# HGRN scores by 64 x 64 blocks on quarters of TensorE's array, kept compact and spread before the output

## The chip, the cores and the metric

The kernel runs on one core of a Trainium2 chip. A core has engines that work side by side: TensorE (PE; its weight loads are PEld in the profile), VectorE (DVE), ScalarE (ACT), GpSimd (POOL), and SyncE (SP), whose queue issues the transfers here. The metric is the device time of one execution in microseconds; the median of several runs is compared.

## The reference

Two layers of an encoder on a sequence of 1024 tokens with 1024 features, in float32. In each layer one combined projection feeds three branches: attention (8 query heads, 2 key heads), a bidirectional HGRN2 recurrence (4 heads with a 64 x 64 state), and a convolution module. Their outputs are concatenated and projected back, and an MLP follows. The change is in the HGRN branch, which for each head and each direction computes

```
S_t = diag(f_t) S_{t-1} + k_t outer v_t
o_t = S_t^T q_t
```

with a forget gate f_t per feature. The forward and the backward result are added, normalised and gated. Within a chunk of tokens the result of one direction is a masked product: the score of query i with key j is the sum over features of q_i k_j times all the f between them, and the output is scores times v.

## The kernel before

The kernel is written for a scheduler that takes the order of the code as priorities and decides the final order of each engine's instructions and the place of every buffer when the program is built. The engines then run these orders as they stand; an instruction at the head of a queue that waits holds all that is behind it.

All activations lie features by tokens: 128 partitions (features) by 1024 tokens. An HGRN tile holds two heads, rows 0 to 63 and rows 64 to 127, so a layer has two objects, `Hgrn(0)` and `Hgrn(1)`, that I call head pair 0 and head pair 1. `Hgrn.__init__` takes its columns of the projection (L223 is the line of all dense matmuls) and leaves q, k and the gates of both directions in `X` (four arrays: key forward in 0, query backward in 1, query forward in 2, key backward in 3) and `T` (the products of f).

`core` is a generator. It doubles the length over which decay is folded in, from 1 token to 128. Ahead of each step s = 2, 4, 8, 16, 32, 64 (`LEVELS`), `scores` computes the scores between the two halves of every block of 2s tokens, for the forward direction in one half of the mask and for the backward one in the other:

- ScalarE (L490) puts the queries and keys of the level together in `qx` and `kx`.
- TensorE (L502) multiplies, for each of eight chunks of 128 tokens and each of the two heads, a full 128 x 128 block from the head's 64 rows. Of it only the pairs of that level are wanted. The eight chunks are done in two halves, each into a pair of PSUM banks, one bank for each head. Head pair 0 takes "c" banks for the first half and "e" banks for the second; head pair 1 takes the two "e" banks both times.
- VectorE merges each bank into the score array `A` (two heads x 8 chunks x 128 queries) under the level's mask: L509 (a product) on the first level, L513 (a predicated copy) on the others.

After that GpSimd and VectorE fold the gates of this length into `X` (L533) and `T` (L534). When all levels are done, TensorE turns the keys (L547), ScalarE copies them out (L548), `U` gathers the products of keys and values per chunk (L557), VectorE runs the states over the chunks (L566), and L591 adds, for each chunk, scores times values and states times queries.

Head pair 0 is interleaved with the projections of attention's q, k and v (`qkv`, L223) and with the convolution's taps on VectorE (L357). Head pair 1 is interleaved with attention: one step of its generator after every second unit of 64. A unit is a head and 128 queries: scores on TensorE (L753), a scaled reduction on VectorE (L764), the exponential on ScalarE (L767), a division on GpSimd (L769), flips on TensorE (L790) which ScalarE and VectorE copy out (L794, L795), and value matmuls (L811), which take one of the same two "e" banks for four units at a time. L199 and L200 split the weights of the dense matmuls into two parts; L819 copies values out of a bank.

Of the kernel before, what the change touches and what calls it, by code (L numbers as in the profile page):

```python
# [17 lines left out]
P = 128  # L18
# [27 lines left out]
def tile_hybrid_trunk(  # L46
# [56 lines left out]
    def pse():  # L103
        return psum.t([P, 512], "e", bufs=2)
# [8 lines left out]
    cons = cst.t([P, 260], "cons")  # L113
    masks = cst.t([P, len(LEVELS), P], "masks", dt=U8)
    ident = cons[:, 0:128]
# [176 lines left out]
    for l in range(DEPTH):  # L292
# [114 lines left out]
        class Hgrn:  # L407
# [76 lines left out]
            def scores(self, lev):  # L484
# [3 lines left out]
                for dst, arrs in ((qx, (1, 2)), (kx, (0, 3))):  # L488
                    for hf in range(2):
                        nc.scalar.activation(  # L490
                            dst.rearrange("p (n h s) -> p n h s", h=2, s=s)[:, :, hf],
                            X[:, arrs[hf]].rearrange("p (n h s) -> p n h s", h=2, s=s)[:, :, hf],
                            AF.Copy,
                        )
                for g in range(2):
                    scs = [pse(), pse()] if g == 1 or self.ls == 1 else [psc(), psc()]
                    for q in range(4):
                        c = g * 4 + q
                        cs = slice(c * P, (c + 1) * P)
                        for hh in range(2):  # L500
                            rows = slice(64 * hh, 64 * hh + 64)
                            nc.tensor.matmul(  # L502
                                scs[hh][:, q * P : (q + 1) * P], kx[rows, cs], qx[rows, cs], start=True, stop=True
                            )
                    for hh in range(2):
                        dst = self.A[:, hh, g * 4 : g * 4 + 4, :]
                        src = scs[hh].rearrange("p (a b) -> p a b", a=4)
                        if lev == 0:
                            nc.vector.tensor_tensor(  # L509
                                dst, src, masks[:, 0].unsqueeze(1).to_broadcast([P, 4, P]), op=ALU.mult  # L510
                            )
                        else:
                            nc.vector.copy_predicated(  # L513
                                dst, masks[:, lev].unsqueeze(1).to_broadcast([P, 4, P]), src
                            )
                    yield

            def core(self):
                ls, X, T, vt = self.ls, self.X, self.T, self.vt
                self.A = hg.t([P, 2, 8, P], "A")  # L520
                yield from self.near()
# [30 lines left out]
                for d in range(2):  # L552
                    U = pse()
                    for c in range(8):
                        for hh in range(2):
# [3 lines left out]
                                start=True, stop=True,  # L559
                            )  # L560
                    step = 1 if d == 0 else -1
                    c = 0 if d == 0 else 7
# [9 lines left out]
                for g in range(2):  # L572
                    op = pse()
                    for q in range(4):
                        c = g * 4 + q
                        cs = slice(c * P, (c + 1) * P)
                        for i in range(3):
                            for hh in range(2):
                                rows = slice(64 * hh, 64 * hh + 64)
                                dst = op[rows, q * P : (q + 1) * P]  # L580
                                if i == 0:
                                    a, b = vt[:, c, rows], self.A[:, hh, c, :]
                                elif i == 1:
# [32 lines left out]
        if l == 0:  # L616
            mraw = x8((P, len(LEVELS), P))
            nc.sync.dma_start(mraw, mask_d)
            nc.vector.tensor_copy(masks, mraw)
# [600 lines left out]
def host_layout(inputs):  # L1220
# [37 lines left out]
    for ax, pos in ((0, t // 64), (1, t % 64)):  # L1258
        ang = (inv[:, None] * pos[None, :].astype(np.float32)).astype(np.float32)
        cs, sn = np.cos(ang.astype(np.float64)), np.sin(ang.astype(np.float64))  # L1260
        for hd in range(2):
            b = hd * 64 + ax * 32
            rope[0, b : b + 16], rope[0, b + 16 : b + 32] = cs, cs
            rope[1, b : b + 16], rope[1, b + 16 : b + 32] = -sn, sn
    i = np.arange(P)
    masks = np.zeros((P, len(LEVELS), P), np.float32)
    for n, s in enumerate(LEVELS):
        same = (i[:, None] // (2 * s)) == (i[None, :] // (2 * s))
        diff = (i[:, None] // s) != (i[None, :] // s)
        masks[:, n] = same & diff  # L1270
    return {
# [21 lines left out]
```

## Time and profile before

| | |
|---|---|
| median of 3 runs | 2533.78 us (2532.68 to 2536.23) |
| the profiled execution | 2533.45 us |
| its span, first to last instruction | 2531.70 us |
| TensorE busy | 2455.4 us (97%) |
| VectorE busy | 2003.8 us (79%) |
| ScalarE busy | 1204.2 us (48%) |
| head pair 0, levels, layer 1 and 2 | 125 to 220 and 1387 to 1482 us |
| head pair 1, levels, layer 1 and 2 | 337 to 470 and 1597 to 1731 us |

In the lines of the profile an instruction is named by its line in the kernel, its engine, what it writes and what it reads. The length of a matmul's record includes the time through the array, so neighbours overlap; the time that one really takes is the distance from one start to the next. A float32 score matmul leaves two records, each with a weight load of its own. The chain of waits is followed back from the last instruction, always to what came last.

### The profile page before, as it was taken

The page shows a single profiled execution, that of the slowest core. Times are in us where ns is not written, and L with a number is a line of the kernel's source. Part 1 is how long each engine was busy: PE and PEld are TensorE (multiplying, and loading weights), DVE is VectorE, ACT ScalarE, POOL GpSimd, SP SyncE. Part 2 cuts the span into 40 slices and gives each one's busy share as a digit, 9 for nine tenths or more (in the row PEclk, how much of TensorE's full clock was granted, in tenths as well). Part 3 has the DMA queues.
Part 4 walks back from the last instruction along what each step waited for, and adds up shares of the span by engine and source line. Part 5 has one row for each costly group of instructions (what it writes and reads, how often), then busy time and mean ns, then how long its engine had stood idle before and what let it go on. Part 6 is the DMA issues. An engine that isn't in the chain of part 4 may idle for free. (4 is left out here: it accounts for less than half of the span.)

```text
span 2531.7 us, 34044 instructions
## 1 busy us (share of the span) xinstructions
PE 2455.4 (97%) x12608; PEld 2017.4 (80%) x12608; DVE 2003.8 (79%) x3051; ACT 1204.2 (48%) x1960; POOL 723.3 (29%) x463
## 2 busy tenths in 40 slices
PE   8999899999999999999999998999999999999999
PEld 7777778878788887888887777788787888878887
DVE  6999689862887778987859995998638877789886
ACT  4222478763544444443523215787635444444332
POOL 0232556533034330000123225564330344200000
PEclk9999999999999999999999999999999999999999
DMA  4102300032254458554221113000322444574442
GB/s 163 55 34 71 104 17 18 26 119 90 91 179 142 150 175 298 163 175 158 76 100 42 45 60 104 18 20 24 133 92 89 169 140 163 186 280 158 162 151 91
DMA packets 113077, 286.99 MB, mean 113 GB/s; under 512 B 11408, under 2 KB 11664, under 8 KB 112912
## 3 DMA queue, kind: packets, MB, share of 16 engines
q1 hardware_dynamic: 112912, 284.83, 32.5%
q8 instruction: 99, 1.62, 0.3%
q14 instruction: 66, 0.54, 0.1%
HBM read 197.75 MB, written 87.03 MB: 112 GB/s over the span
## 5 line engine op out<-in xcount | busy, mean ns | idle before, releaser
L223 PE MATMUL S<-xs,whi 128*128 128x512 f32 x1280 | 361.1, 402 | 8.7 <-ACT whi L199 7.4
L223 PEld LDWEIGHTS S<-xs,whi 128*128 128x128 f32 x1280 | 241.0, 191 | 63.8 <-ACT whi L199 7.4
L1204 PE MATMUL S<-xs,xs 128*128 128x512 f32 x816 | 201.6, 390 | 2.6 <-DVE xs L905 2.6
L223 PE MATMUL S<-xs,wlo 128*128 128x512 f32 x640 | 201.9, 396 | 0.0
L904 ACT ACTIVATE xs<-m 128x512 fp32r<-128x512 f32 x216 | 126.0, 619 | 141.7 <-DVE m L915 48.8
L769 POOL TENSOR_SCALAR P<-P,mx 128x1024 f32<-128x1024 f32 x124 | 141.3, 1140 | 163.0 <-DVE mx L768 116.0
L795 DVE TENSOR_TENSOR PT<-c,PT 128x512 fp32r<-128x512 f32 x256 | 170.5, 683 | 21.1 <-ACT PT L794 19.6
L1204 PEld LDWEIGHTS S<-xs,xs 128*128 128x128 f32 x816 | 152.8, 188 | 35.4 <-DVE xs L905 3.4
L794 ACT ACTIVATE PT<-c 128x512 fp32r<-128x512 f32 x256 | 148.4, 592 | 68.3 <-PE c L790 65.1
L357 DVE SCALAR_TENSOR_TENSOR x<-x,par,x 128x1009 f32<-128x1009 f32 (+14 forms) x120 | 172.3, 1436 | 1.6
L811 PE MATMUL e<-PT,x 128*128 128x256 f32 x1024 | 170.8, 297 | 1.4 <-ACT PT L794 1.1
L199 ACT ACTIVATE whi<-raw 128x1024 fp32r<-128x1024 f32 x56 | 59.1, 1057 | 233.0 <-PE S L223 214.0
L764 DVE TENSOR_SCALAR_CACHE_REDUCE P<-S,nqc 128x1024 f32<-128x1024 f32 x124 | 158.6, 1279 | 14.1 <-PE S L753 10.1
L790 PE MATMUL c<-cons,P 128*128 128x128 f32 x992 | 152.0, 277 | 12.0 <-POOL P L769 7.1
L905 DVE TENSOR_TENSOR xs<-m,xs 128x512 fp32r<-128x512 f32 x216 | 144.7, 693 | 22.1 <-ACT xs L904 22.0
L753 PE MATMUL S<-x,QS 128*128 128x512 f32 x480 | 152.1, 419 | 8.1 <-DVE P L764 7.9
L767 ACT ACTIVATE P<-P,mx 128x1024 f32<-128x1024 f32 x124 | 142.4, 1148 | 28.0 <-DVE P L764 25.8
L261 POOL TENSOR_TENSOR tmp<-tmp,tmp 128x1024 f32<-128x1024 f32 x19 | 50.7, 2666 | 361.4 <-ACT tmp L260 361.2
L811 PEld LDWEIGHTS e<-PT,x 128*128 128x128 f32 x1024 | 137.2, 191 | 11.1 <-ACT PT L794 3.4
L790 PEld LDWEIGHTS c<-cons,P 128*128 128x128 f32 x992 | 113.2, 140 | 40.8 <-POOL P L769 11.9
L223 PEld LDWEIGHTS S<-xs,wlo 128*128 128x128 f32 x640 | 122.1, 191 | 26.7 <-issue 0.4
L1204 PE MATMUL e<-xs,xs 128*128 128x512 f32 x552 | 141.0, 390 | 1.3 <-ACT xs L904 0.9
(310 smaller groups left out, 5632.7 us busy)
## 6 DMA issues: line engine op xcount, KB each, us to landing
m<-ad SPq DMA_DIRECT2D x104, 512.0 KB, 3.8
ad<-x SPq DMA_DIRECT2D x176, 256.0 KB, 2.2
raw<-w_in_t SPq DMA_DIRECT2D x40, 512.0 KB, 3.4
xs<-w_t SPq DMA_DIRECT2D x36, 512.0 KB, 3.7
raw<-w_t SPq DMA_DIRECT2D x36, 512.0 KB, 3.6
m<-w_t SPq DMA_DIRECT2D x32, 512.0 KB, 6.7
ad<-tmp SPq DMA_DIRECT2D x48, 256.0 KB, 2.1
x<-w_t SPq DMA_DIRECT2D x24, 512.0 KB, 4.8
```

The source lines that it names most:

```text
L223: nc.tensor.matmul(zp[h] if type(zp) is list else zp[:, h, :], w, xx[:, h * 512 : (h + 1) * 512], start=first, stop=last)
L357: nc.vector.scalar_tensor_tensor(y[:, lo:hi], u[:, lo + d : hi + d], par[:, l, wof + tap : wof + tap + 1], y[:, lo:hi], op0=ALU.mult, op1= ...
L753: nc.tensor.matmul(S[:, hb, :], qs, kk[:, hb * 512 : (hb + 1) * 512], start=first, stop=not first)
L764: nc.vector.tensor_scalar(Pt, S, nqc[:, j, ci : ci + 1], 3.0e38, op0=ALU.mult, op1=ALU.min, accum_out=mx[:, 1:2])
L767: nc.scalar.activation(Pt, Pt, AF.Exp, bias=mx[:, 1:2], scale=-1.0, accum_out=mx[:, 2:3])
L769: nc.gpsimd.tensor_scalar(Pt, Pt, mx[:, 3:4], 0.0, op0=ALU.mult, op1=ALU.add)
L790: nc.tensor.transpose(t[:, q * P : (q + 1) * P], Pt[:, hb, q * P : (q + 1) * P], ident)
L794: nc.scalar.activation(hi, src, AF.Copy)
L795: nc.vector.tensor_tensor(lo, src, hi.bitcast(F32), op=ALU.subtract)
L811: nc.tensor.matmul(pvp[:, cs], VS[g][:, hb * 4 + kb, :], pt[:, kb, :], start=hb == 0 and n == 0, stop=hb == 1 and n == 7,)
L905: ordered("v", nc.vector.tensor_tensor(lo, src, hi.bitcast(F32), op=ALU.subtract))
L1204: nc.tensor.matmul(banks[dt], w[i][:, dt * P : (dt + 1) * P], a[j], start=n == 0 and name not in ("M6", "M7", "M3"), stop=n == 3 * SG - 1, ...
```

## The change

A block of 128 x 128 scores holds four blocks of 64 x 64. For s below 64 all wanted pairs lie in the two diagonal blocks, for s = 64 in the two others. The new `scores` multiplies only these: 64 keys by 64 queries, out of the 64 rows of one head. The key half b decides the output partitions (64 b), so head and half together choose one of four quarters of the array, and the code goes through them in the order (0,0), (1,1), (0,1), (1,0) of head and half. The result of a chunk has 64 columns instead of 128, so the eight chunks of a head fill one bank, where they filled two; one pair of banks is held over both halves of the level, and is merged after the second. Head pair 0 takes a "c" and an "e" bank, head pair 1 the two "e" banks.

`A` is compact: place 0 for the diagonal blocks, place 1 for the others. VectorE merges the levels 2 to 32 into place 0; for 64 ScalarE copies to place 1 without a mask. `spread`, called once for each head after that direction's `U` matmuls, lays both places out as 128 columns a chunk in `X[:, 0]` and `X[:, 3]`, whose keys have been turned by then, with four ScalarE copies of 64 rows. The output matmuls read these. The mask of the last level goes, and the others have 64 columns.

```diff
+                def part(sc, hh, c, b):
+                    rows = slice(64 * hh, 64 * hh + 64)
+                    k0 = c * P + 64 * b
+                    q0 = c * P + 64 * (b if s < 64 else 1 - b)
+                    nc.tensor.matmul(
+                        sc[64 * b : 64 * b + 64, c * 64 : (c + 1) * 64], kx[rows, k0 : k0 + 64], qx[rows, q0 : q0 + 64],
+                        start=True, stop=True,
+                    )
+
+                def merge(sc, hh):
+                    src = sc.rearrange("p (a b) -> p a b", a=8)
+                    if s == 64:
+                        nc.scalar.activation(self.A[:, 1, hh], src, AF.Copy)
+                        return
+                    dst = self.A[:, 0, hh]
+                    mask = masks[:, lev].unsqueeze(1).to_broadcast([P, 8, 64])
+                    if lev == 0:
+                        nc.vector.tensor_tensor(dst, src, mask, op=ALU.mult)
+                    else:
+                        nc.vector.copy_predicated(dst, mask, src)
+
+                scs = [pse(), pse()] if self.ls == 1 else [psc(), pse()]
                 for g in range(2):
-                    scs = [pse(), pse()] if g == 1 or self.ls == 1 else [psc(), psc()]
...
+                    for c in range(4 * g, 4 * g + 4):
+                        for hh, b in ((0, 0), (1, 1), (0, 1), (1, 0)):
+                            part(scs[hh], hh, c, b)
+                    if g == 1:
                         for hh in range(2):
-                            rows = slice(64 * hh, 64 * hh + 64)
-                            nc.tensor.matmul(
-                                scs[hh][:, q * P : (q + 1) * P], kx[rows, cs], qx[rows, cs], start=True, stop=True
-                            )
...
+                            merge(scs[hh], hh)
                     yield
+
+            def spread(self, hh):
+                dst = self.X[:, 3 * hh].rearrange("p (c b q) -> p c b q", b=2, q=64)
+                for b in range(2):
+                    rows = slice(64 * b, 64 * b + 64)
+                    nc.scalar.activation(dst[rows, :, b], self.A[rows, 0, hh], AF.Copy)
+                    nc.scalar.activation(dst[rows, :, 1 - b], self.A[rows, 1, hh], AF.Copy)
...
-                self.A = hg.t([P, 2, 8, P], "A")
+                self.A = hg.t([P, 2, 2, 8, 64], "A")
...
+                    self.spread(d)
...
-                                    a, b = vt[:, c, rows], self.A[:, hh, c, :]
+                                    a, b = vt[:, c, rows], X[:, 3 * hh, cs]
...
-            mraw = x8((P, len(LEVELS), P))
+            mraw = x8((P, len(LEVELS) - 1, 64))
```

The lines of the changed kernel are shifted: its score matmuls are L500, its merges L513 (first level), L515 and, on ScalarE, L508; the spreading copies L531 and L532; attention's scores L770, its flips L807, its value matmuls L828.

The built orders differ in these places. First TensorE beside attention in layer 1, at one level of head pair 1: `e` with a number is a PSUM bank of scores or of values, `m` are `kx` and `qx`, `c` a bank for flips. Before:

```order
L790 MATMUL c_2948<-cons_77,P_2829 128x128 x4
L502 MATMUL e_2955<-m_467_2862,m_466_2861 128x128 x4
L753 MATMUL S_488_2967<-x_269_1811,QS_2741 128x512 x2
L753 MATMUL S_488_2967<-x_270_1812,QS_2741 128x512 x2
L790 MATMUL c_2978<-cons_77,P_2885 128x128 x4
L811 MATMUL e_2843<-PT_2852,x_156_991 128x256
L811 MATMUL e_2843<-PT_2853,x_156_991 128x256
L811 MATMUL e_2843<-PT_2852,x_156_991 128x256
L502 MATMUL e_2956<-m_467_2862,m_466_2861 128x128 x4
```

The four matmuls of one head (`e_2955`) and the four of the other (`e_2956`) stand apart; in between the value matmuls go on in the bank `e_2843`. In the change, at the third level:

```order
L807 MATMUL c_3282<-cons_77,P_3158 128x128 x4
L500 MATMUL e_3234<-m_506_3229,m_505_3228 64x64
L807 MATMUL c_3302<-cons_77,P_3197 128x128 x4
L500 MATMUL e_3234<-m_506_3229,m_505_3228 64x64 x6
L500 MATMUL e_3235<-m_506_3229,m_505_3228 64x64 x15
L500 MATMUL e_3234<-m_506_3229,m_505_3228 64x64
L500 MATMUL e_3235<-m_506_3229,m_505_3228 64x64
L770 MATMUL S_525_3345<-x_257_1891,QS_3188 128x512 x2
L770 MATMUL S_525_3345<-x_258_1892,QS_3188 128x512
L807 MATMUL c_3320<-cons_77,P_3197 128x128 x4
L770 MATMUL S_525_3345<-x_258_1892,QS_3188 128x512
L807 MATMUL c_3356<-cons_77,P_3258 128x128 x4
```

Here too one head comes after the other, each now in a longer run that goes back and forth between the two column halves; 16 value matmuls of the next group follow behind the last row. Next TensorE beside the projections in layer 1, in the change, at the fourth level: `c_1225` and `e_1226` are its two heads.

```order
L223 MATMUL S_163_1071<-xs_145,wlo_784 128x512 x2
L500 MATMUL c_1225<-m_177_1220,m_176_1219 64x64 x8
L223 MATMUL S_185_1254<-xs_103,whi_909 128x512 x2
L223 MATMUL S_185_1254<-xs_104,whi_909 128x512 x2
L223 MATMUL S_185_1254<-xs_103,wlo_910 128x512 x2
L500 MATMUL c_1225<-m_177_1220,m_176_1219 64x64 x8
```

The 16 matmuls of `e_1226` stand in one row further down, and the fifth level is laid out likewise; on the other four levels rows of `c` and `e` alternate one by one. Last VectorE in the same stretch, where the first level is merged: `wlo` is the low part of a weight tile and `tmp` a projection's result. Before:

```order
L327 TENSOR_TENSOR tmp_898<-S_132_788,Rb_307 128x1024
L509 TENSOR_TENSOR A_777<-c_886,masks_78 128x512
L509 TENSOR_TENSOR A_777<-c_887,masks_78 128x512
L200 TENSOR_TENSOR wlo_904<-raw_901,whi_903 128x1024
L509 TENSOR_TENSOR A_777<-e_915,masks_78 128x512
L509 TENSOR_TENSOR A_777<-e_916,masks_78 128x512
L533 TENSOR_TENSOR X_465<-X_465,T_466 128x64x8 x2
```

There are four merges, and a weight split stands behind the first two. In the change:

```order
L327 TENSOR_TENSOR tmp_904<-S_132_788,Rb_307 128x1024
L200 TENSOR_TENSOR wlo_910<-raw_907,whi_909 128x1024
L513 TENSOR_TENSOR A_777<-c_886,masks_78 128x512
L513 TENSOR_TENSOR A_777<-e_887,masks_78 128x512
L549 TENSOR_TENSOR X_465<-X_465,T_466 128x64x8 x2
L550 TENSOR_TENSOR T_466<-T_466 128x128
```

The two merges that remain stand behind the weight split.

More of the change, by code (lines that the diff above doesn't have):

```diff
@@ L113, in tile_hybrid_trunk @@
     cons = cst.t([P, 260], "cons")
-    masks = cst.t([P, len(LEVELS), P], "masks", dt=U8)
+    masks = cst.t([P, len(LEVELS) - 1, 64], "masks", dt=U8)
     ident = cons[:, 0:128]
@@ L495, in scores @@
+                scs = [pse(), pse()] if self.ls == 1 else [psc(), pse()]
                 for g in range(2):
-                    scs = [pse(), pse()] if g == 1 or self.ls == 1 else [psc(), psc()]
-                    for q in range(4):
-                        c = g * 4 + q
-                        cs = slice(c * P, (c + 1) * P)
+                    for c in range(4 * g, 4 * g + 4):
+                        for hh, b in ((0, 0), (1, 1), (0, 1), (1, 0)):
+                            part(scs[hh], hh, c, b)
+                    if g == 1:
@@ L500, in scores @@
                         for hh in range(2):
-                            rows = slice(64 * hh, 64 * hh + 64)
-                            nc.tensor.matmul(
-                                scs[hh][:, q * P : (q + 1) * P], kx[rows, cs], qx[rows, cs], start=True, stop=True
-                            )
[L505 to L515, printed above, removed]
@@ L1264, in host_layout @@
             rope[1, b : b + 16], rope[1, b + 16 : b + 32] = -sn, sn
[L1265 to L1270, printed above, removed]
+    i = np.arange(P)[:, None]
+    j = 64 * (i // 64) + np.arange(64)[None, :]
+    masks = np.zeros((P, len(LEVELS) - 1, 64), np.float32)
+    for n, s in enumerate(LEVELS[:-1]):
+        masks[:, n] = (i // (2 * s) == j // (2 * s)) & (i // s != j // s)
     return {
```

## The prediction

> **What bounds the kernel now.** I read the page first, then the busy times of the four stretches in which HGRN scores are made, then the chain of waits inside two of them, and last single runs of score matmuls in the timeline. The page says that TensorE is nearly always busy and VectorE four fifths of the time:
>
> ```profile
> PE 2455.4 (97%) x12608; PEld 2017.4 (80%) x12608; DVE 2003.8 (79%) x3051; ACT 1204.2 (48%) x1960; POOL 723.3 (29%) x463
> ```
>
> Averages hide the stages, so here are the stretches: head pair 0 of layer 1 and layer 2 (95 us each, beside the projections) and head pair 1 of both layers (133 and 134 us, beside attention).
>
> ```profile
> core 0: us, PE busy (x) PEld busy (x) DVE busy (x) ACT busy (x) POOL busy (x), PEclk, DMA share, GB/s
> 125.00:220.00 95.00, 89.28 (x576) 72.34 (x576) 92.02 (x133) 28.59 (x42) 34.93 (x18) 0.98 0.14 48
> 337.00:470.00 133.00, 128.73 (x871) 108.97 (x870) 119.02 (x216) 102.63 (x182) 76.53 (x64) 1.00 0.07 19
> 1387.00:1482.00 95.00, 89.69 (x590) 73.45 (x589) 89.13 (x136) 26.27 (x38) 31.84 (x16) 0.95 0.14 48
> 1597.00:1731.00 134.00, 129.63 (x879) 109.93 (x878) 120.00 (x218) 103.56 (x184) 76.96 (x64) 1.00 0.06 19
> ```
>
> Beside the projections VectorE is busy for 92.0 of 95 us in layer 1, TensorE for 89.3: VectorE leads and TensorE follows closely. Beside attention it is the other way round, 128.7 and 119.0 of 133 us. The chain of waits tells which of the two is on the path. It reaches back only to 1414.85 us, so I have it for the later 67.2 us of the projection stretch of layer 2 (its shares are of the 95 us) and for the whole attention stretch of layer 2:
>
> ```profile
> by line: PE S L223 15.1%; DVE x L357 11.6%; PE e L502 6.1%; PE e L162 5.7%; DVE tmp L631 4.7%; issue 4.6%; DVE A L513 3.7%; DVE nwy L156 2.8%; DVE tmp L632 2.5%; PE e L557 2.3%; PE c L502 1.7%; DVE tmp L629 1.5%; DVE X L533 1.3%; PE c L547
> 1414.85 1.07 POOL X L533
> ```
>
> ```profile
> by line: PE c L790 19.1%; PE e L811 18.8%; PE e L502 17.3%; PE S L753 16.3%; POOL P L769 5.5%; issue 5.5%; DVE P L764 2.7%; DVE PT L795 2.7%; DVE X L533 2.4%; POOL X L533 2.1%; POOL QS L743 2.0%; POOL x L821 1.0%; DVE A L509 1.0%; ACT P L76
> ```
>
> In the projection stretch the VectorE lines that are shown sum to 28.1% of 95 us, 26.7 of 67.2 us: 40% of the chain is VectorE's queue, and the score matmuls (L502, 6.1 + 1.7%) are 7.4 us, 11% of it. In the attention stretch the path is TensorE: its four lines are 71.5%, and L502 alone is 17.3% of 134 us, 23.2 us. Both engines that the change relieves are therefore on the path, each in its own stage.
>
> **The matmuls.** A score matmul leaves two records. Here are a run beside the projections (the heads alternate), two runs there back to back, a run beside attention (one head alone), and a run of L557, whose 64-column outputs alternate between the column halves; the columns are start, length, engine, line.
>
> ```profile
> 131.79 1.16 PE L502 MATMUL c<-m,m 64*128 64x128 f32 x16
> 132.88 1.19 PE L223 MATMUL S<-xs,whi 128*128 128x512 f32 x4
> ```
>
> ```profile
> 198.46 1.16 PE L502 MATMUL c<-m,m 64*128 64x128 f32 x16
> 199.45 1.06 PE L502 MATMUL e<-m,m 64*128 64x128 f32 x16
> 200.44 0.73 PE L223 MATMUL S<-xs,wlo 128*128 128x512 f32 x2
> ```
>
> ```profile
> 410.74 1.16 PE L502 MATMUL e<-m,m 64*128 64x128 f32 x8
> 411.82 0.66 PE L790 MATMUL c<-cons,P 128*128 128x128 f32 x4
> ```
>
> ```profile
> 215.76 1.15 PE L557 MATMUL e<-vt,T 128*64 128x64 f32 x32
> 216.85 0.96 PE L223 MATMUL S<-xs,whi 128*128 128x512 f32 x3
> ```
>
> From start to start: alternating heads 1.09 us for 16 records, 68 ns each; one head alone 1.08 us for 8, 135 ns; column halves 1.09 us for 32, 34 ns. Two matmuls on different row halves overlap, two in one row half do not, and with 64 columns on alternating column halves a record costs a quarter of 135 ns. The change doubles the records (32 instead of 16 matmuls a level, 384 instead of 192 records a stretch), each with 64 weight columns and 64 moving columns.
>
> Beside attention the built order still has one head at a time in most places, so its runs alternate the column halves of one row half. The nearest row is L557 at 34 ns (it uses all rows, the new one half of them): 192 x 135 = 25.9 us become 384 x 34 = 13.1 us, 49% less. Of the 23.2 us on the chain that takes 11.5. I take 10 per layer: waits for GpSimd (L769, 5.5%) stay, and VectorE, at 119.0 of 133 us, would be next if it were not relieved too. The bounds are 13 (all of it, and the 1.3 us of L509 on the chain) and 5 (VectorE or L769 is late next).
>
> The Trainium skill, TensorE: Matmul & The Clock Gate, Part 3, says that a weight load overlaps a running matmul only where the row group differs; by that rule a single head's run gains nothing from its column halves and these 10 us are 0. L557 does not agree: its weight loads have the same rows each time, and a record takes 34 ns, a quarter of what a row half alone takes with twice the columns.
>
> Beside the projections the heads do alternate, so all four quarters are in use. The row bounds are 34 ns a record (four overlap no better than two), where 384 x 34 = 13.1 us equal the 192 x 68 = 13.1 of now, and 17 ns (they overlap twice as well), where 6.5 us go. I take the middle, 3.3 us of 13.1, 25%; of the 7.4 us on the chain, scaled from 67.2 to 95 us to 10.5, that is 2.6, and two levels of the new order run one head after the other, so 2. The Trainium skill, the same page, Back-to-back issue gap, gives about 25 ns as the least distance of two matmuls; by it 384 records take 9.6 us, an estimate that lies between the two bounds, and no row here is that short.
>
> **The merges.** Removed are half of VectorE's merges and all those of the 64 level:
>
> ```profile
> L509 DVE TENSOR_TENSOR A<-e,masks x12: 673/684/692, 143.2 to 1614.2; 128x512 f32<-128x512 f32 x12
> L509 DVE TENSOR_TENSOR A<-c,masks x4: 674/674/678, 140.9 to 1398.8; 128x512 f32<-128x512 f32 x4
> L513 DVE COPY_PREDICATED A<-masks,e x60: 709/736/757, 149.9 to 1730.4; 128x512 f32<-128x512 uint8 x60
> L513 DVE COPY_PREDICATED A<-masks,c x20: 710/724/741, 146.1 to 1462.1; 128x512 f32<-128x512 uint8 x20
> ```
>
> These 96 are 24 a stretch; 10 remain (two heads, five levels), over the same 512 elements a partition. Fourteen go: 2 of L509 at 0.68 and 12 of L513 at 0.73 us, 10.1 us of VectorE a stretch. Beside the projections VectorE is 40% of the chain, so 4.0 us come back directly. The lower bound is 14/24 of what L513 itself has on the chain (3.7% of 95, 3.5 us), 2 us; the upper one is all 10.1, if each stall of TensorE there goes back to that queue. With the matmuls the stretch gains 4 + 2 = 6 per layer, between 1 (the lower 2 less what a worse order may cost) and 10 (what the matmuls add beyond that I do not count). Beside attention the merges' 10.1 us only keep VectorE from being next. The smaller mask saves some of one 553 ns cast in the whole program; I cost it at nothing.
>
> **What is added.** ScalarE gets two copies from PSUM for the 64 level and eight spreading copies, L531 and L532, a stretch. Nearest are L548 for the former and L819 (64 rows, 512 elements) for the latter; the last rows are the stretches after head pair 1's levels, where the spreading falls:
>
> ```profile
> L548 ACT ACTIVATE T<-c x16: 574/598/622, 209.6 to 1750.7; 128x512 f32<-128x512 f32 x16
> L819 ACT ACTIVATE tmp<-e x32: 592/594/598, 330.1 to 1822.4; 64x512 f32<-64x512 f32 x32
> 470.00:520.00 50.00, 49.76 (x426) 41.25 (x424) 39.36 (x84) 39.85 (x72) 25.53 (x22) 1.00 0.10 33
> ```
>
> That is 2 x 0.598 + 8 x 0.594 = 5.9 us. Beside the projections ScalarE is busy for 28.6 of 95 us; the copies stand ahead of the next weight split (L199) in its queue and are hidden by its idle time. After the levels of head pair 1 it is busy for 39.9 of 50 us and also copies the turned softmax blocks (L794) that TensorE's value matmuls need; there a spreading copy in front of such a copy delays it by up to 0.6 us. Nothing to 4 us (most of the 4.8 us of eight copies shows); TensorE is at 49.8 of 50 us there with other work queued, so I take 1 per layer. The output matmuls read the spread scores instead of A and wait for the spreading. The rows of layer 1 show the second U run and the first output:
>
> ```profile
> 219.79 1.15 PE L557 MATMUL e<-vt,T 128*64 128x64 f32 x32
> ...
> 228.12 0.44 PE L591 MATMUL e<-A,vt 128*64 128x128 f32 x4
> ```
>
> The 8.3 us between them, in which VectorE runs the states, cover the 4.8 us of spreading; without that cover it would be within the same 4 us.
>
> **The banks.** Now one pair of PSUM banks is held from the first half of a level to its merge, instead of a pair for each half. Beside attention both are "e" banks, and value matmuls (L811) want one of the same two. In the queue behind a value matmul that waits are the flips and scores of the next units, and for those ScalarE and VectorE wait. Before, this is what TensorE waited for in that stretch of layer 1:
>
> ```profile
> PE c L790 <- POOL P L769: 3.1, 6, 0.8
> PE c L790 <- DVE PT L795: 0.5, 2, 0.3
> PE e L811 <- ACT PT L794: 0.2, 1, 0.2
> PE S L753 <- DVE P L764: 0.2, 1, 0.2
> PE e L502 <- ACT m L490: 0.2, 1, 0.2
> ```
>
> ```profile
> L764 DVE TENSOR_SCALAR_CACHE_REDUCE P<-S,nqc 128x1024 f32<-128x1024 f32 x124 | 158.6, 1279 | 14.1 <-PE S L753 10.1
> ```
>
> No value matmul waits for a merge (L764 is given for the third rival), although the pair is taken twice a level; the new order takes it once a level and still fills the other bank's time with value matmuls of the group before. I cost it at nothing, up to the price in the third rival.
>
> **The sum.** Per layer 10 + 6 - 1 = 15 us, so 30 for two. The profiled execution took 2533.45 us, 1.75 more than its span of 2531.70, and lies 0.33 below the median of 2533.78. 2533.45 - 30 is 2503.45; against the median it is 2504. The bounds per layer are 13 + 10 - 0 = 23 and 5 + 1 - 4 = 2, that is 2488 and 2530.
>
> **The rivals.**
>
> First, column halves in one row half do not overlap. A record of 64 columns then costs half of 135 ns, 68, and 384 of them 26.1 us: beside attention nothing is gained from TensorE. Beside the projections the row halves overlap as now, and nothing is gained either. What is left is 4.0 us of merges beside the projections, 1 beside attention, less 1: 4 per layer, 2525.5. L557 speaks against it; for it, that no row shows two column halves with the rows of only one half. It is what the rule that I took from the Trainium skill, TensorE: Matmul & The Clock Gate, Part 3, would make of this change.
>
> Second, the other side: a record costs a fixed time per row half, whatever its columns, because of the turn from one load to the next in the same rows. At 135 ns 384 records take 51.8 instead of 25.9 us beside attention and at 68 ns 26.1 instead of 13.1 beside the projections: 39 us more a layer, less 4 from the merges and with the 1 from ScalarE, 36, so 2533 + 72, 2606. It starts to lose where a record of one head alone takes over about 75 ns: 384 x 75 = 28.8, 2.9 more than now, and 1.4 more beside the projections at the same ratio, eat the 4.0 of the merges. L557, 34 ns with two loads in each of the same rows, speaks against it; only a cost that comes with half rows speaks for it.
>
> Third, the pair of "e" banks beside attention: its merges come late in VectorE's queue, so that a value matmul waits on each level for two merges (1.5 us) and one softmax reduction ahead of them (L764, 1.3): 2.8 x 6 = 17 us a layer, which takes the 15 away and 2 more, 2538. It decides only if TensorE has nothing left that does not need a bank. The waits above speak against it. For it: the order has places where 16 value matmuls follow a level at once, so the group has been held back.
>
> **How the numbers follow.** My forecast has 0.74, the rivals 0.10, 0.07 and 0.09. The predicted time is the forecast's, 2504. The range runs from its lower bound, rounded to 2487, to 2531, which takes in the first rival and its own upper bound; outside are the second rival, most of the third, and a tail, together about 0.2. About 0.2%, 5 us, can be told from no change here. Faster by more than that: the forecast but for a tail of 0.02, and 0.08 of the first rival, 0.80. Within it: the tail, the rest of the first rival, and 0.05 of the third, 0.09. Slower: the second rival and 0.04 of the third, 0.11.
>
> **What would show it.** In the new profile the score matmuls (L500) should have 1536 records of about 34 ns from start to start beside attention and 17 to 34 beside the projections; the attention stretch, from the first to the last score, should be near 123 instead of 133 us and the projection stretch near 89 instead of 95, with VectorE's merges at 40. 68 ns beside attention would show the first rival, 100 and more the second, and value matmuls (L828) that wait for a VectorE merge the third. If score matmuls got cheaper as said and the attention stretch did not shrink, the step from TensorE's work to the chain is wrong.

## The result and the profile after

The changed kernel takes 2518.61 us (median of 6 runs, 2516.18 to 2520.18), the kernel before, beside it, 2533.76 (6 runs). The ratio is 0.9936 [0.9923, 0.9949], so the change makes the kernel 0.64% faster, 15.2 us. The forecast was 2504, 30 us. The sign and the range held; half of the gain is missing. The six runs agree within 0.2%, so the missing half is not noise.

The profiled execution took 2518.79 us, with a span of 2517.0. First the busy times of its page:

```profile
PE 2442.2 (97%) x13376; PEld 1992.3 (79%) x13376; DVE 1964.1 (78%) x2995; ACT 1225.9 (49%) x2000; POOL 728.2 (29%) x463
```

TensorE lost 13.2 us and VectorE 39.7. VectorE's part is the forecast's own: 14 merges fewer in each of four stretches are 40.4 us. The shares do not move, so the stages again (length, then PE, PEld, DVE, ACT, POOL busy, clock, DMA): head pair 0, head pair 1, and both in layer 2.

```profile
125.00:215.00 90.00, 87.39 (x777) 69.82 (x778) 80.78 (x121) 33.85 (x53) 38.12 (x18) 0.94 0.15 51
335.00:460.00 125.00, 119.01 (x1067) 101.19 (x1066) 110.71 (x204) 104.26 (x186) 76.99 (x65) 0.99 0.07 20
1380.00:1470.00 90.00, 87.39 (x784) 70.15 (x784) 83.01 (x119) 33.21 (x52) 32.95 (x17) 0.92 0.14 51
1580.00:1710.00 130.00, 123.57 (x1105) 104.63 (x1104) 116.93 (x211) 109.45 (x196) 82.11 (x68) 1.00 0.08 22
```

Beside the projections the two engines have changed places: VectorE was busy for 92.0 of 95 us and is now for 80.8 of 90, TensorE for 89.3 of 95 and now for 87.4 of 90. Next the score matmuls, the merges and half of the spreading copies (L531) of the changed kernel, by line and tile (minimum, median and maximum duration in ns, first and last start):

```profile
L500 PE MATMUL e<-m,m x1152: 218/218/367, 131.7 to 1708.3; 64*64 64x64 f32 x192
L500 PE MATMUL c<-m,m x384: 218/218/366, 131.7 to 1451.8; 64*64 64x64 f32 x192
...
L513 DVE TENSOR_TENSOR A<-e,masks x6: 670/676/679, 142.6 to 1600.2; 128x512 f32<-128x512 f32 x6
L513 DVE TENSOR_TENSOR A<-c,masks x2: 677/678/679, 142.0 to 1394.6; 128x512 f32<-128x512 f32 x2
...
L515 DVE COPY_PREDICATED A<-masks,e x24: 727/734/761, 146.7 to 1687.0; 128x512 f32<-128x512 uint8 x24
L515 DVE COPY_PREDICATED A<-masks,c x8: 715/726/745, 146.1 to 1437.4; 128x512 f32<-128x512 uint8 x8
...
L531 ACT ACTIVATE X<-A x16: 617/627/636, 207.6 to 1741.5; 64x512 f32<-64x512 f32 x16
```

There are 1536 records and 40 merges, as said. The rates stand in the timeline of TensorE; the first run lies beside the projections, the second beside attention.

```profile
131.67 0.27 PE L500 MATMUL c<-m,m 64*64 64x64 f32 x1
131.67 0.27 PE L500 MATMUL e<-m,m 64*64 64x64 f32 x1
...
131.77 0.22 PE L500 MATMUL c<-m,m 64*64 64x64 f32 x1
...
131.83 0.22 PE L500 MATMUL c<-m,m 64*64 64x64 f32 x1
...
132.29 1.19 PE L223 MATMUL S<-xs,whi 128*128 128x512 f32 x4
...
416.27 1.15 PE L500 MATMUL e<-m,m 64*64 64x64 f32 x32
417.35 0.74 PE L828 MATMUL e<-PT,x 128*128 128x256 f32 x4
```

Beside attention 32 records take 1.08 us, 34 ns each, exactly L557's rate before. In the trace they start in pairs 7 ns apart, a pair every 58 ns: the two column halves work side by side. Beside the projections 32 take 0.62 us, 19 ns: four quarters start within 20 ns, the next four after about 100 ns, and from there four more every 60 ns. The start of a run costs extra, and most runs are shorter than 32. Summed over a stretch, each run from its first start to the next matmul's start (or to its own end, where TensorE then idles), head pair 1's scores fell from 27.3 to 16.5 and 16.1 us, 43 ns a record, and head pair 0's from 15.6 and 17.9 to 10.9 and 11.0. So a full run has the rate of the forecast or a better one, but beside attention TensorE is relieved of 11 us and not of the 12.8 that the forecast worked out. On the chain of waits in the attention stretch of layer 2 the scores fell from 17.3% to 9.9%:

```profile
by line: PE c L807 19.0%; PE e L828 18.1%; PE S L770 16.2%; PE e L500 9.9%; issue 7.1%; POOL P L786 7.0%; POOL X L549 4.2%; DVE P L781 3.7%; POOL x L838 2.8%; DVE PT L812 1.9%; ACT P L784 1.9%; ACT PT L811 1.8%; DVE T L550 1.7%; DVE X L549 
```

So where is the other half? I divided the span at the starts of four groups: the first score of head pair 0, the first value matmul of attention, the last score, the last value matmul, and the first MLP product. Two of these groups, value matmuls and scores of layer 1 in the kernel before and after, with first and last start:

```profile
L811 PE MATMUL e<-PT,x x512: 274/283/685, 313.7 to 560.8; 128*128 128x256 f32 x171
L502 PE MATMUL e<-m,m x192: 272/272/373, 338.0 to 468.4; 64*128 64x128 f32 x192
```

```profile
L828 PE MATMUL e<-PT,x x512: 276/283/682, 311.9 to 552.1; 128*128 128x256 f32 x171
L500 PE MATMUL e<-m,m x384: 218/218/366, 335.8 to 458.4; 64*64 64x64 f32 x192
```

| us, layer 1 / layer 2 | before | after | difference | E1 (below) | E1 to before |
|---|---|---|---|---|---|
| first score to first value matmul | 181.9 / 186.7 | 180.2 / 177.9 | -1.7 / -8.8 | 177.2 / 177.6 | -4.7 / -9.1 |
| first value matmul to last score | 154.7 / 154.4 | 146.5 / 145.6 | -8.2 / -8.8 | 146.6 / 145.5 | -8.1 / -8.9 |
| last score to last value matmul | 92.4 / 92.7 | 93.7 / 93.6 | +1.3 / +0.9 | 93.5 / 94.0 | +1.1 / +1.3 |
| to the first MLP product (output projection) | 82.1 / 82.1 | 84.2 / 84.2 | +2.1 / +2.1 | 82.1 / 82.0 | 0 / -0.1 |
| MLP and the rest | 745.3 / 627.6 | 748.5 / 630.9 | +3.2 / +3.3 | 746.8 / 625.4 | +1.5 / -2.2 |

The first three rows give 25.3 us back. The last two lose 10.7. From the last value matmul of a layer to the next layer's first score, or to the end, the order on TensorE is the same before and after. The reason stands in single matmuls of the MLP (timeline of TensorE, start, length, line, tiles), first before:

```profile
2054.23 2.88 PE L1003 MATMUL S<-xs,wlo 128*128 128x512 f32 x12
2056.95 2.88 PE L1003 MATMUL e<-m,whi 128*128 128x512 f32 x12
2059.67 2.88 PE L1003 MATMUL c<-m,wlo 128*128 128x512 f32 x12
```

and after, where the same line is L1020:

```profile
2056.08 2.88 PE L1020 MATMUL S<-xs,whi 128*128 128x512 f32 x12
2058.80 2.96 PE L1020 MATMUL e<-m,wlo 128*128 128x512 f32 x12
2061.60 2.96 PE L1020 MATMUL c<-m,whi 128*128 128x512 f32 x12
```

Twelve matmuls took 2.72 us from start to start, 227 ns each. With `xs` as moving tile they still do; with `m` they take 2.80, 233 ns. No instruction of these was edited, but an address was: the mask tile shrank from 768 to 320 bytes a partition, and every tile that lies behind it on the same side, the weights `whi` and `wlo` and `xs` among them, moved down by 448 bytes. `m` and `mx` lie on the other side and stayed.

### The profile page after: what moved, and what is told of

It is laid out like the page before. It is cut to its first block, busy times and chain, and to the rows that moved or that the text cites. A ratio compares the mean times of both kernels' runs of the same rounds, so it can differ in the third digit from the quotient of the medians.

```text
span 2517.0 us, 35561 instructions
## 1 busy us (share of the span) xinstructions
PE 2442.2 (97%) x13376; PEld 1992.3 (79%) x13376; DVE 1964.1 (78%) x2995; ACT 1225.9 (49%) x2000; POOL 728.2 (29%) x463
## 4 chain that ended last, share of the span: by engine, by line
PE 79%; DVE 12%; issue 3%; ACT 3%; POOL 2%; DMA 0%; SPq 0%; POOLq 0%; DVEq 0%; ACTq 0%
PE S L223 17%; PE S L1221 10%; PE c L1020 10%; PE S L1020 7%; PE e L1020 7%; PE e L1221 7%; PE c L1221 6%; PE e L828 3%; DVE x L357 3%; PE c L807 3%; PE S L770 3%; PE e L162 1%; PE e L500 1%; PE e L608 1%; DVE P L781 1%
## 5 line engine op out<-in xcount | busy, mean ns | idle before, releaser
L828 PE MATMUL e<-PT,x 128*128 128x256 f32 x1024 | 173.6, 299 | 1.5 <-ACT tmp L837 0.8
L781 DVE TENSOR_SCALAR_CACHE_REDUCE P<-S,nqc 128x1024 f32<-128x1024 f32 x124 | 158.5, 1278 | 15.8 <-PE S L770 11.3
L807 PE MATMUL c<-cons,P 128*128 128x128 f32 x992 | 152.4, 277 | 16.1 <-POOL P L786 11.5
L770 PE MATMUL S<-x,QS 128*128 128x512 f32 x480 | 153.1, 418 | 10.2 <-DVE P L781 9.1
L807 PEld LDWEIGHTS c<-cons,P 128*128 128x128 f32 x992 | 113.7, 141 | 45.2 <-POOL P L786 16.7
L828 PEld LDWEIGHTS e<-PT,x 128*128 128x128 f32 x1024 | 138.9, 193 | 9.3 <-ACT PT L811 2.6
```

Of the source, the lines that this page charges most:

```text
L770: nc.tensor.matmul(S[:, hb, :], qs, kk[:, hb * 512 : (hb + 1) * 512], start=first, stop=not first)
L781: nc.vector.tensor_scalar(Pt, S, nqc[:, j, ci : ci + 1], 3.0e38, op0=ALU.mult, op1=ALU.min, accum_out=mx[:, 1:2])
L807: nc.tensor.transpose(t[:, q * P : (q + 1) * P], Pt[:, hb, q * P : (q + 1) * P], ident)
L828: nc.tensor.matmul(pvp[:, cs], VS[g][:, hb * 4 + kb, :], pt[:, kb, :], start=hb == 0 and n == 0, stop=hb == 1 and n == 7,)
```

## The experiments

**The theory** is that the address distance between a matmul's weights and its moving tile sets its rate, and that this took the missing half. **The rival** is that the dense stages only came to lie otherwise in time against transfers and other engines. After that, each term of the forecast is tested by adding its cost back.

### E1: the changed kernel, all tiles at their old addresses

```diff
-    masks = cst.t([P, len(LEVELS) - 1, 64], "masks", dt=U8)
+    masks = cst.t([P, 768], "masks", dt=U8)[:, 0:320].rearrange("p (a b) -> p a b", b=64)
```

> The changed kernel with its mask tile padded from 320 to 768 bytes a partition, so that every tile behind it lies where it lay before the change; every engine's order of instructions is that of the changed kernel. Theory (address): the change gained about 27 us up to the end of attention and lost about 12 us in the output projection and the MLP, because the weight tiles moved by 448 bytes against the moving tiles of the other end of SBUF (m, mx). Then 12 matmuls that move m take 2.72 instead of 2.80 us again, 100 us of the first MLP product hold 443 matmuls instead of 436, and the time is 2506, between 2503 and 2509. Rival (phase): the MLP is slower because it starts at another phase of the clock gate or of the transfers, or because the run differs; then nothing changes, 2518 to 2519, with 2.80 us.

Measured: 2504.10 us (4 runs, 2503.94 to 2504.65), ratio 0.9874 [0.9852, 0.9896]. The order of every engine is that of the changed kernel. In the timeline of TensorE the `m` rows are back at 2.72:

```profile
2047.31 2.88 PE L1020 MATMUL e<-m,wlo 128*128 128x512 f32 x12
2050.03 2.88 PE L1020 MATMUL c<-m,whi 128*128 128x512 f32 x12
```

The same shows in the output projection, whose moving tile is `mx`: the 448 matmuls with `whi` have records of 395 ns on average in the changed kernel and of 390 ns in E1.

The time is in the expected range (2503 to 2509), and the rival falls. 448 bytes of padding are worth 14.5 us by the medians. The working: 448 + 224 matmuls with `mx` and 1344 with `m`, 2016 in all, times 80 / 12 = 6.7 ns are 13.4 us. For the output projection alone it is 672 x 6.7 = 4.5 us, and the table has 2.1 + 2.2. The last two rows of the table together have 11.5 us; another 3.0 lie in layer 1's projection stretch, where the granted clock differs too (see further down), so not all of the 14.5 is shown to be the address.

### E2: the kernel before, with only the weights moved

Half of the mask tile goes behind the weight tiles, so that `raw`, `whi` and `wlo` lie 384 bytes lower and all else stays.

```diff
+    mk = Pool("mk")
-    for p in (dram, psum, cst, wp, sp_):
+    for p in (dram, psum, cst, wp, mk, sp_):
...
-    masks = cst.t([P, len(LEVELS), P], "masks", dt=U8)
+    masks = cst.t([P, 3, P], "masks", dt=U8)
+    masks2 = mk.t([P, 3, P], "masks2", dt=U8)
```

> The kernel before, with half of its masks moved to a tile behind the weight tiles: raw, whi and wlo lie 384 bytes lower, everything else where it was. Theory (address): all float32r matmuls whose weights are in whi or wlo and whose moving tile is elsewhere go from 227 to 233 ns: about 1920 of the dense projections and 1344 of the first MLP product, 6.6 ns each, 21 us, less what the projections hide: 2549 to 2556. Rival (phase): 2532 to 2536, at 227 ns.

Measured: 2557.97 us (2556.34 to 2561.44), ratio 1.0088 [1.0068, 1.0108]. A kernel without any of the change, slower by 0.9%, 22.7 us more than the kernel before beside it (2535.23); the theory had 21, and the time lies 2 us above its range. Now `xs` as moving tile is slow too, since it no longer moves along with the weights:

```profile
2053.20 2.96 PE L1006 MATMUL e<-xs,wlo 128*128 128x512 f32 x12
2056.00 2.96 PE L1006 MATMUL S<-xs,whi 128*128 128x512 f32 x12
```

In the changed kernel `xs` had moved by the same 448 bytes as the weights and stayed fast, and `m` had stayed and became slow. So neither tile's place alone decides; the distance of the two does.

### E3, E4, E5: three other distances

The mask tile of E1 with 512, 704 and 640 bytes, which puts the weights 256, 64 and 128 bytes below their old place; each was run once. The edit of E3 (the others have 704 and 640 in the place of 512):

```diff
-    masks = cst.t([P, 768], "masks", dt=U8)[:, 0:320].rearrange("p (a b) -> p a b", b=64)
+    masks = cst.t([P, 512], "masks", dt=U8)[:, 0:320].rearrange("p (a b) -> p a b", b=64)
```

> The changed kernel with the mask tile padded to 512 bytes, so that the weight tiles are 256 bytes off where they were before the change. If what counts is the distance of the two reads modulo 256 or less, 12 matmuls that move m take 2.72 us and the time is about 2506; if modulo 512 or more, 2.80 us and about 2518. Rival (phase): no relation, about 2518.

> The changed kernel with the mask tile padded to 704 bytes: 64 bytes off. If any distance that is no multiple of the row counts, 2.80 us for 12 matmuls that move m and about 2518; if 64 bytes are one unit, 2.72 us and about 2506. Rival (phase): about 2518.

> The changed kernel with the mask tile padded to 640 bytes: the weight tiles lie 128 bytes below where they lay before the change. Shifts of 448 and 384 were slow, 256 was fast, 64 in between. If the distance counts modulo 256, 128 is as far off as it can be: 2.80 us for 12 matmuls that move m, and 2516 to 2520. If 128 bytes are a unit and 384 was slow for another reason, 2.72 us and 2504 to 2508.

Measured: 2507.79, 2511.46 and 2520.76 us. The timelines of E3, E4 and E5:

```profile
2050.28 2.88 PE L1020 MATMUL e<-m,wlo 128*128 128x512 f32 x12
2053.00 2.88 PE L1020 MATMUL c<-m,whi 128*128 128x512 f32 x12
```

```profile
2053.33 2.93 PE L1020 MATMUL e<-m,wlo 128*128 128x512 f32 x12
2056.09 2.91 PE L1020 MATMUL c<-m,whi 128*128 128x512 f32 x12
```

```profile
2061.63 2.96 PE L1020 MATMUL e<-m,wlo 128*128 128x512 f32 x12
2064.43 2.96 PE L1020 MATMUL c<-m,whi 128*128 128x512 f32 x12
```

So 0 and 256 bytes of shift give 2.72 us, 64 give 2.76, and 128, 384 and 448 give 2.80. That fits a pattern that repeats every 256 bytes; if it does, the sign matters, because 448, which is 64 short of two periods, is slower than 64. E4's 2.76 is neither of the two values that were expected. The pattern rests on these six distances, and how the memory brings it about is not shown.

All further kernels are E1 with one more edit, so that the address stays out of the comparison. A difference to E1 is one of medians that were taken apart from each other; the kernel before had 2533.31 to 2535.23 us beside them, so some 2 us of it are open. Each is also built anew, and the scheduler then orders TensorE otherwise than in E1 (834 of 13376 instructions stand in another place in E7, 1022 in E8, 206 in E10), so a difference holds the edit together with its order.

### E6: every score matmul of head pair 1 twice

```diff
-                    nc.tensor.matmul(
+                    for _ in range(2 if self.ls == 1 else 1):
+                        nc.tensor.matmul(
```

> The padded kernel (2504.1 us) with every score matmul of head pair 1 issued twice, so that TensorE's score work beside attention is what it was before the change (768 records of 34 ns, 26 us a layer, instead of 13). The forecast's term: TensorE's score work is on the path there and is worth about 10 us a layer, so 2524, between 2514 and 2530. Rival (VectorE bounds the attention stretch, and the gain there came from its merges): 2504 to 2509.

Measured: 2529.49 us (10 runs, 2527.28 to 2533.53), ratio 0.998 [0.9967, 0.9992], 25.4 above E1. The added work is 384 x 34 ns = 13.1 us a layer, 26.1 in all: nearly all of it shows, and the time is within the expected 2514 to 2530. Value matmuls and scores of layer 1 in E1 and in E6:

```profile
L828 PE MATMUL e<-PT,x x512: 274/283/682, 308.9 to 549.0; 128*128 128x256 f32 x171
L500 PE MATMUL e<-m,m x384: 218/218/366, 332.7 to 455.5; 64*64 64x64 f32 x192
```

```profile
L829 PE MATMUL e<-PT,x x512: 274/283/682, 308.8 to 561.1; 128*128 128x256 f32 x171
L501 PE MATMUL e<-m,m x768: 218/218/267, 332.9 to 466.9; 64*64 64x64 f32 x192
```

From the first value matmul to the last score it is 158.1 instead of 146.6 us (158.0 instead of 145.5 in layer 2). TensorE is the path beside attention; that step holds.

### E7 and E8: the removed merges put back, beside the projections and beside attention

Each merge is repeated until a stretch has the old 24 (E8; E7 has `self.ls == 0`).

```diff
-                            merge(scs[hh], hh)
+                            for _ in range((2 if lev < 4 else 4 if lev == 4 else 1) if self.ls == 1 else 1):
+                                merge(scs[hh], hh)
```

> The padded kernel with the merges of head pair 0 repeated, 24 instead of 10 a layer on VectorE. The forecast's term: the merges beside the projections are worth 4 us a layer, between 2 and 10: 2512, between 2508 and 2524. Rival (the projection stretch was bound by TensorE, and its gain came from the quarters): 2503 to 2507.

> The padded kernel with the merges of head pair 1 repeated, 24 instead of 10 a layer on VectorE, as many as before the change. The forecast's term: the merges beside attention are worth 0 to 1 us a layer, 2504 to 2507. Rival (VectorE bounds the attention stretch): up to 10 us a layer, 2512 to 2524.

E8 measured 2515.37 us (2513.49 to 2515.92), ratio 0.9919 [0.9898, 0.994], 11.3 above E1: 5.6 a layer, where the forecast gave nothing to 1. The time lies outside the forecast's range and in the rival's. Value matmuls and scores of layer 1 in E8:

```profile
L829 PE MATMUL e<-PT,x x512: 274/283/682, 309.6 to 554.5; 128*128 128x256 f32 x171
L500 PE MATMUL e<-m,m x384: 218/218/268, 333.9 to 459.2; 64*64 64x64 f32 x192
```

From the first value matmul to the last one it is 244.9 instead of 240.1 us (layer 2: 244.6 and 239.5). Without the fewer merges some 5 of the 7.0 and 7.6 us that this part had gained are lost again; what is left against the kernel before (247.1 in both layers) is 2.2 and 2.5 us. Part of the loss comes by the banks, as the third rival had it. TensorE's value matmuls in this stretch of E8 (busy time and mean ns, then what ended their idle time):

```profile
L829 PE MATMUL e<-PT,x 128*128 128x256 f32 x271 | 46.1, 296 | 2.9 <-DVE A L515 2.4 <-ACT tmp L838 0.5
```

They wait 2.4 us for a merge (2.3 in layer 2), which they do not in E1. So with cheap scores VectorE is next there, partly through the bank that its merges hold.

E7 measured 2531.76 us (2528.80 to 2536.33), ratio 0.9993 [0.9979, 1.0007], 27.7 above E1: 13.8 a layer, where the forecast had 4 with bounds of 2 and 10.1. Value matmuls of layer 1 in E7:

```profile
L829 PE MATMUL e<-PT,x x512: 274/283/682, 323.2 to 562.3; 128*128 128x256 f32 x171
```

This is above both ranges. The first value matmul starts 14.3 us later than in E1, although the merges add 10.1 us of VectorE, and it starts 9.5 later than in the kernel before, which has the same number. The levels themselves, from the first score to the last, are 2.1 and 3.8 us shorter than in E1; all of the loss comes behind them, where the scheduler had decided another order. There, from 195 to 323 us, TensorE's longest wait is for a result of VectorE:

```profile
PE S L771 <- DVE m L327: 7.1, 1, 7.1
```

In layer 2 it is 6.9 us, in E1 0.4. The granted clock behind the levels is 0.90 and 0.91, where E1 has 0.98. So the added VectorE work does come onto the path, but behind the levels, and the size of that term is not measured by this kernel.

### E9: every score matmul of head pair 0 twice

The edit of E6 with `self.ls == 0`:

```diff
-                    nc.tensor.matmul(
+                    for _ in range(2 if self.ls == 0 else 1):
+                        nc.tensor.matmul(
```

> The padded kernel with every score matmul of head pair 0 issued twice: TensorE's score work beside the projections goes from about 7 to about 14 us a layer, what it was before the change. The forecast's term: 2 us a layer, 2508, between 2504 and 2512. Rival (TensorE bounds the projection stretch): 6 us a layer, 2514 to 2518.

Measured: 2529.41 us, but from 2516.09 to 2533.13 over 10 runs, ratio 0.9976 [0.9959, 0.9992], 25.3 above E1. The expected range ended at 2512 and the rival's at 2518. The added work is 384 x 19 ns = 7.3 us a layer at the rate of four quarters; summed over the runs as above it is 8.6 and 8.8. The profiled run shows +14.2 in layer 1 and +7.1 in layer 2 up to the first value matmul, of which 8.1 and 6.4 lie within the levels, so nearly all of the added work shows there. The rest of layer 1's lies behind the levels, where the granted clock is 0.94 (E1 0.98). TensorE is therefore on the path beside the projections, and the forecast's 2 us for it is too small; how much too small stays open.

### E10: the spreading copies twice

```diff
                     self.spread(d)
+                    self.spread(d)
```

> The padded kernel (2504.1 us) with the spreading copies issued twice: 16 instead of 8 on ScalarE in each stretch. The forecast's term: a set of eight costs about 1 us a layer, so 2506, between 2504 and 2510. Rival (the copies stand in front of attention's copies and all of their 5 us shows): 2512 to 2514.

Measured: 2517.31 us (2515.78 to 2517.80), ratio 0.993 [0.9914, 0.9947], 13.2 above E1. Value matmuls and scores of layer 1 in E10:

```profile
L829 PE MATMUL e<-PT,x x512: 274/283/685, 309.0 to 556.9; 128*128 128x256 f32 x171
L500 PE MATMUL e<-m,m x384: 217/218/366, 335.0 to 457.7; 64*64 64x64 f32 x192
```

From the last score to the last value matmul it is 99.2 us, where E1 has 93.5 (layer 2: 99.2 and 94.0). The second set costs 5.7 and 5.2 us, all of its eight copies' 5.0 and a little more; the first set, from before to E1, had cost 1.1 and 1.3. With the whole time above the rival's range too, the forecast's price holds for the first set alone. That the first set has used up its cover is argued, not shown: what TensorE waits for longer there is the states on VectorE (L584, 2.8 us), not a spreading copy.

### E11 and E12: the spreading on GpSimd, everywhere and for head pair 1 alone

E11:

```diff
-                    nc.scalar.activation(dst[rows, :, b], self.A[rows, 0, hh], AF.Copy)
-                    nc.scalar.activation(dst[rows, :, 1 - b], self.A[rows, 1, hh], AF.Copy)
+                    nc.gpsimd.tensor_copy(dst[rows, :, b], self.A[rows, 0, hh])
+                    nc.gpsimd.tensor_copy(dst[rows, :, 1 - b], self.A[rows, 1, hh])
```

E12 has ScalarE for head pair 0 and GpSimd for head pair 1:

```diff
+                put = nc.gpsimd.tensor_copy if self.ls == 1 else lambda o, i: nc.scalar.activation(o, i, AF.Copy)
```

> The padded kernel with the spreading copies on GpSimd instead of ScalarE. If ScalarE's queue is what the spreading costs (1.2 us a layer behind head pair 1's levels by the profiles), 2502, between 2500 and 2504. Rival (GpSimd's copies take longer and hold up its divisions, L786): 2505 to 2514.

> The padded kernel with the spreading copies of head pair 1 on GpSimd and those of head pair 0 on ScalarE. With all of them on GpSimd the part from the last score to the end of attention was 1.8 and 2.1 us shorter than in the padded kernel, and the projection stretch of layer 1 4.0 longer. If these two are separate, the time is 2500, between 2498 and 2503. Rival (the loss in the projection stretch was the clock's phase and comes or goes by chance): anything up to 2510.

E11 measured 2513.42 us (2509.68 to 2518.62), ratio 0.9918 [0.9901, 0.9934]. From the last score to the last value matmul it is 91.7 and 91.9 us, 1.8 and 2.1 less than E1, but up to the first value matmul it takes 5.0 and 1.4 more. E12 measured 2503.67 us (2502.89 to 2505.69), ratio 0.9885 [0.9867, 0.9902]: 91.8 and 92.0 in that part, yet 1.1 and 0.5 more ahead of the first value matmul, so it is level with E1 (2504.10) and just above its expected 2498 to 2503. E11 is outside the range of its theory and in its rival's. E12 and E1 beat the kernel before by 30 us and the changed kernel by 14.5; of the two I would take E1, which has the smaller edit.

## Why the prediction was right, and the step that failed

**The step that failed** is the last sentence on the merges: "The smaller mask saves some of one 553 ns cast in the whole program; I cost it at nothing." As work it is nothing. As 448 bytes that go ahead of other tiles it cost 13.4 us by the count of slowed matmuls and 14.5 by the medians (2518.61 against E1's 2504.10). Nothing in the rest of the sum had a place for it, because the sum went through instructions, and no instruction of the dense stages was edited. That 2518.61 lies within the range all the same is luck: the range was meant for other stages and other causes.

**The other terms** are tested against E1, where that cost is gone. The forecast of 2504 is then its median, which is partly luck: one term was too large and another too small.

- Attention stretch, predicted 10 a layer: 8.1 and 8.9. That TensorE is on the path there is shown by E6, the 34 ns by the timeline; short runs leave 11 us of relief where 12.8 were worked out. What was wrong is that VectorE's merges were costed as a mere guard: in E8, with its own order, the old merges take 3.0 and 4.3 of this back, and about 5 up to the last value matmul, so their removal is a part of the gain and the matmuls alone would not have brought it.
- Projection stretch, predicted 6: 4.7 and 9.1. The term was rather too small: over this part the granted clock is 0.98 before and 0.96 in E1 in layer 1, and 0.95 in both in layer 2. Set right for that, as an estimate, layer 1 gains 4.7 + 177.2 x 0.04 - 181.9 x 0.02 = 8.2 us. That VectorE's work comes onto the path is seen in E7's wait, that TensorE is on it in E9. The split into 4 for the merges and 2 for the matmuls is not borne out: put back one at a time, each costs more than both were said to bring. E7, with the cheap matmuls and the old merges, needs 191.8 and 192.3 us for this part, E9, with the fewer merges and more work on TensorE, 191.4 and 184.7, where the kernel before had 181.9 and 186.7 and E1 177.2 and 177.6. So the two terms do not add; that each relief needs the other is argued from these two kernels, whose orders differ.
- A record on four quarters, taken as the middle of 34 and 17 ns: 19, nearly the lower bound. The Trainium skill, TensorE: Matmul & The Clock Gate, Back-to-back issue gap, has about 25 ns as the least distance of two matmuls; four quarters together, at 19 ns, go below it here.
- Spreading, predicted 1: 1.1 and 1.3, with the limit that E10 shows.
- Banks, predicted 0: no value matmul waits for a merge in the attention stretch of the changed kernel, and the third rival falls. In E8, with the merges back, one does.

**The first two rivals** fall with the 34 ns and the pairs that start 7 ns apart: two column halves of one row half do overlap. The rule from the Trainium skill, TensorE: Matmul & The Clock Gate, Part 3, that a load overlaps only another row group, does not describe these matmuls. The changed kernel lies 7 us under the first rival's 2525.5, but that is chance: it has the gain of the forecast and another loss.

**Layer 1's projection stretch** gained 1.7 us in the changed kernel and 4.7 in E1, which has the same order. The granted clock differs there. Two windows of the changed kernel, in which TensorE is busy for 4.40 and all 5 of 5 us:

```profile
255.00:260.00 5.00, 4.40 (x24) 3.95 (x24) 2.42 (x3) 2.56 (x3) 0.00 (x0) 0.69 0.88 288
260.00:265.00 5.00, 5.00 (x17) 4.11 (x18) 1.31 (x2) 3.88 (x4) 0.00 (x0) 0.63 0.32 115
```

In E1 the clock is 1.00 in both. These windows lost 5 x 0.31 + 5 x 0.37 = 3.4 us of full clock, against 3.0 us of difference. E3, whose order on TensorE is again the same, has 0.66 in both windows and takes 180.3 us for this part, like the changed kernel's 180.2. That the clock is the cause is argued from these three executions; no kernel was made for it, and why the clock fell in two of them is open.

## What to carry to other kernels

When a change resizes a tile, look at which tiles move, and compare the start-to-start distance of matmuls in stages that were not edited; padding a tile to its old size separates the edit from its side effect in one run. A range that holds is no proof of the sum behind it: test the terms one by one. When an edit relieves two engines of one stage, cost the stage by what is left of the slower one, not by a sum of shares of the chain. When a gain is missing, divide the span at the starts of a few groups first: here that pointed to the stages without any edit.

## What the runs showed of the hardware that I had not expected

- A matmul of 128 x 512 takes 227 or 233 ns, 2.9% more, by the distance between its weights' and its moving tile's addresses: 2.72 us for twelve at a shift of 0 and 256 bytes, 2.76 at 64, 2.80 at 128, 384 and 448.
- Four quarters of the array take 64 x 64 float32 records at 19 ns each, two column halves of one row half at 34, a row half alone with 128 columns at 135. These are rates of full runs; with short runs between other matmuls the 384 records beside attention took 43 ns each.
